# The mixed MLP stage: the fourth block product two block products later, and the seven seats for raw weights dealt three, two and two

## The chip, the cores and the metric

The kernel runs on one core of a Trainium2 chip. The metric is the device time of one execution in microseconds; of several runs the median is taken. The engines are named by their jobs: TensorE (PE in the profile) multiplies matrices, VectorE (DVE) and ScalarE (ACT) work on elements, GpSimd (POOL) and SyncE (SP) here mostly issue transfers. Each engine takes its instructions in the order of its own queue.

## What is computed

One layer of an encoder trunk on 256 tokens of width 2048, in float32: a mixer (three attention-like branches behind one projection), and then the MLP, which is the part that matters here:

```python
hdn = jnp.square(jax.nn.relu(_rms_norm(x, norm_mlp_pre[l]) @ w_mlp_up[l]))
x = x + _rms_norm(hdn @ w_mlp_down[l], norm_mlp_post[l])
```

`w_mlp_up` is 2048 by 8192 and `w_mlp_down` 8192 by 2048. All weights are read once from memory as a stream of blocks of 128 partitions by 1024 float32 (512 KB).

## The kernel before

**Products in split precision.** TensorE multiplies in a rounded format. So each raw weight block is split in two: ScalarE copies it to a rounded `hi` (line 158 or 1379), and VectorE subtracts `hi` from the raw block to get `lo` (159 or 1380). The other operand is split likewise. A product is then three sets of matmuls: `hi` by `hi`, `hi` by `lo`, `lo` by `hi`.

**Up and down halves of the MLP.** The up half makes "heads" of 128 hidden units each. A head takes two half blocks of weights (function `up`: 16 matmuls each, lines 174 to 182, 2.77 us of TensorE), after which `post` brings it through relu and square. Two heads make a pair `m`. The function `forms` makes, of a finished pair, the seven sums and differences that the down half needs, as tiles `fm` (16 buffers, lines 1439 to 1450). For the last eight heads `split3` makes a plain split instead (1461, 1462).

**Block products.** For most of the hidden units the down half multiplies two by two blocks with seven products instead of eight (function `down`). The unit is a quad: four heads by 1024 output columns, with the weight blocks called 11, 12, 21 and 22. The products are called F1 to F7, six matmuls each (lines 1517 to 1519), and each needs one weight block or a sum of blocks. `prep` gets them in this order:

- F3 loads 22 and 12, splits 22, and adds 12 into 22 (VectorE, line 1476).
- F7 loads 11, splits 22 as it then is, adds 11 into 22 (VectorE) and issues a transfer on GpSimd's queue that adds 11 into 12 (`dma_add`, line 1479).
- F1 splits 11.
- F6 loads 21, splits 22, and issues a GpSimd transfer that adds 21 into 22.
- F2 splits 21, F5 splits 12, and F4 splits 22 with all four in it.

F4 is thus the last reader of 22, and waits for the second GpSimd transfer of its quad. The products of one group of quads add up in PSUM banks `Q` (F3, F7, F1 in the ring of four `gps` banks that the heads use too, the others in the ring `mps`). When the last quad of a group is done, `post` of `down` moves them into the result `y` through tiles `junk` (line 1524). There are eight groups, of three or four quads: 28 quads.

**The order of the work.** The mixed stage weaves the heads of the up half, four half blocks a quad at first and at the end sometimes three or two (the list `share`), between the products. The order within a quad is written out by hand in the loop at the end of `hybrid_block`: a list of items, among them `us[0]` to `us[3]` (half blocks), `last4` (F4 of the quad before) and `"old"` (finished pairs whose forms are handed over to the list of small tasks). The driver `drive` does the `prep` of an item two products ahead of its matmuls, and emits two small tasks behind each half block and none behind a product. TensorE's order is this order; on the other engines and queues the framework orders instructions by when it expects them to be ready.

**Where raw blocks lie.** The raw blocks of `down` have seats. The function `seat` has two buffers for each of three roles: 22, 12 and 11. A seventh seat is half of a spare tile, `spare[1][:, 0]`, called `sp` in the profile. The function `braw` (line 1360 on) picks the seat and issues the load on SP's queue (line 1369). Before the change 22 and 12 have two seats each, and 11 and 21 together take turns on three: two of role 11 and the spare one (the counter `made`). A load waits until the block that had its seat has been read for the last time. The half blocks of the up weights are loaded on the same SP queue, into a ring of three buffers called `raw` (line 145).

Of the kernel before, what the change touches and what calls it, by code (L numbers as in the profile page):

```python
# [10 lines left out]
F32 = mybir.dt.float32  # L11
# [39 lines left out]
def hybrid_block(ctx, tc, xt, x, gains, params, consts, lora, gup, wst, out):  # L51
# [13 lines left out]
    def nm(s):  # L65
        uid[0] += 1
        return f"{s}_{uid[0]}"
# [7 lines left out]
    def pk():  # L75
        return pkpool.tile([128, 512], F32R, tag="pk", name=nm("pk"), bufs=24)
# [1144 lines left out]
    def seat(role, dt):  # L1221
        return p2.tile([128, HALF], dt, tag=f"raw{role}", name=nm(f"raw{role}"), bufs=2)
# [72 lines left out]
    for k2 in range(0, KT, 2):  # L1295
        turned(k2, 1)
        src = [trs[k2 // 2][:, i * T:i * T + T] for i in range(2)]
        us = [pk(), pk()]
# [29 lines left out]
    ahead, spare, made, kinds, units = [AHEAD], [], [0], [0], [0]  # L1328
# [31 lines left out]
    def braw(h0, c0, n):  # L1360

        i, j = int(n[0]) - 1, int(n[1]) - 1
        u = base + 64 * (h0 // 16) + 32 + 8 * (c0 // 512 + j) + h0 % 16 // 2
        if n in ("22", "12"):
            raw = seat(int(n), F32)
        else:
            made[0] += 1
            raw = seat(11, F32) if made[0] % 3 else spare[1][:, 0]
        nc.sync.dma_start(out=raw.rearrange("p (r c) -> p r c", r=2),
                          in_=wst[u:u + 2, :, 512 * i:512 * i + 512].rearrange("r p c -> p r c"))  # L1370
        return raw
# [62 lines left out]
    def forms(m):  # L1434

        def sums():
            h = hid[m]
            s = hid[m, 1] = p2.tile([128, 4, 128], F32, tag="sfm", name=nm("sfm"), bufs=1)
            V.tensor_tensor(s[:, 0:2], h[:, 0:4:2], h[:, 3:4].to_broadcast([128, 2, 128]), ALU.subtract)
            V.tensor_tensor(s[:, 2], h[:, 0], s[:, 1], ALU.add)  # L1440
            V.tensor_tensor(s[:, 3], s[:, 2], h[:, 1], ALU.subtract)
            fmh[m] = fm()
            A.activation(fmh[m][:, 0:3], h[:, 0:3], AF.Copy)
            A.activation(fmh[m][:, 3:7], s, AF.Copy)

        def low():
            h, s, hi = hid.pop(m), hid.pop((m, 1)), fmh[m]
            lo = fml[m] = fm()
            V.tensor_tensor(lo[:, 0:3], h[:, 0:3], hi[:, 0:3].bitcast(F32), ALU.subtract)
            V.tensor_tensor(lo[:, 3:7], s, hi[:, 3:7].bitcast(F32), ALU.subtract)  # L1450

        return [(("fm", m), sums), (("fm", m), low)]

    def split3(m):

        def half(i):
            h = hid[m]
            t = fm().rearrange("p a b -> p (a b)")[:, 0:512]
            src = h[:, 0:4:3] if i == 0 else h[:, 1:3]
            hi = t[:, 0:T].rearrange("p (s t) -> p s t", s=2)  # L1460
            A.activation(hi, src, AF.Copy)
            V.tensor_tensor(t[:, T:].rearrange("p (s t) -> p s t", s=2), src, hi.bitcast(F32), ALU.subtract)
            hp[2 * m + i] = t

        return [(("fm", m), lambda i=i: half(i)) for i in range(2)]

    def down(b, sb):
# [13 lines left out]
        def prep(f, d):  # L1481

            h0 = FIRST[b] + 4 * d
            if f == 3:
                R[d, "22"], R[d, "12"] = braw(h0, c0, "22"), braw(h0, c0, "12")
                r = parts(R[d, "22"])
                add(R[d, "22"], R[d, "12"])
            elif f == 7:
                R[d, "11"] = braw(h0, c0, "11")
                r = parts(R[d, "22"])  # L1490
                add(R[d, "22"], R[d, "11"])
                dma_add(R[d, "12"], R[d, "11"])
            elif f == 1:
                r = parts(R[d, "11"])
            elif f == 6:
                R[d, "21"] = braw(h0, c0, "21")
                r = parts(R[d, "22"])
                dma_add(R[d, "22"], R[d, "21"])
            elif f == 2:
                r = parts(R[d, "21"])  # L1500
            elif f == 5:
                r = parts(R[d, "12"])
            else:
                r = parts(R[d, "22"])
            return r
# [56 lines left out]
    def later(new):  # L1562
        return (None, lambda _: urgent.append(lambda: tasks.extend(new)), 0)
# [20 lines left out]
    old = []  # L1584
    last4 = None
# [5 lines left out]
    for b in range(4):  # L1591
        for sb in range(2):
            for d, F in enumerate(down(b, sb)):
                us = [halves.pop(0) for _ in range(share.pop(0))]
                new = [j // 2 for i, (u, j) in enumerate(us) if j % 2 and (u, j) == halves_of[j]]
                us = [u for u, j in us] + [None] * 4
                last = b == 3 and sb == 1 and d == SIZES[3] // 4 - 1
                for it in (F[3], us[0], last4, "old", F[7], F[1], us[1], F[6], F[2], us[2], F[5], us[3]):
                    if it == "old":
                        keep = []  # L1600
                        for m in old:
                            if m in left:
                                work.append(later(split3(m) if m >= LAST else forms(m)))
                            else:
                                keep.append(m)
                        old[:] = keep
                    elif it:
                        work.append(it[:2] + (1,) if last and it[2] == 0 else it)
                old.extend(new)
                last4 = F[4]  # L1610
                if sb:
                    for m in (2 * d, 2 * d + 1):
                        left[FIRST[b] // 2 + m + 8] = 0
# [195 lines left out]
```

## Time and profile before

| | |
|---|---|
| median of 3 runs | 1491.31 us (1491.28 to 1491.65) |
| the profiled execution | 1493.0 us, of which the span from first to last instruction is 1491.2 us |
| mean granted TensorE clock | 0.998 |
| memory read, written | 282.65 MB, 4.19 MB |
| loads of raw blocks on SP's queue | 497 of 512 KB, 4.4 us from issue to landing (median) |
| adding transfers on GpSimd's queue | 38 and 18 of 512 KB, 7.4 and 7.6 us |

How to read the lines that follow. A row of a timeline has the start in us, the time in us, the engine, the line of the kernel, the operation, what it writes and reads, and in brackets how long the engine stood idle before it and who ended that. A row of the waits has who waited for whom, the total in us, how often, and the longest. A row of the chain of waits has the start, the time and what it was. A row of a table by stretches has, for a stretch from A to B us, the busy time of each engine with its number of instructions, then the granted clock, the share of the DMA engines and GB/s. Ends of matmuls are modelled and overlap, so gaps on TensorE are measured from start to start.

### The profile page before, as it was taken

The numbers are of one execution on the slowest core, as the hardware profiler recorded it, in microseconds if no ns is written. First come the engines' busy times: TensorE is split into PE (matmuls) and PEld (weight loads), VectorE is DVE, ScalarE is ACT, GpSimd is POOL, SyncE is SP. The second block draws the span as 40 slices with busy tenths as digits, with TensorE's granted clock in tenths as the row PEclk, the third lists the DMA queues.
The fourth block names the chain that finished last, engine by engine and source line by source line (L and its number), as shares of the span: only waits on it lengthen the run. The fifth ranks groups of instructions, "written<-read, shape, count | busy, mean of one in ns | idle before, by whom it ended". The sixth has DMA issues, their size and how long they took to land.

```text
span 1491.2 us, 22865 instructions
## 1 busy us (share of the span) xinstructions
PE 1477.0 (99%) x8427; PEld 1247.7 (84%) x8427; DVE 1214.7 (81%) x1688; ACT 933.1 (63%) x1394; POOL 90.0 (6%) x160
## 2 busy tenths in 40 slices
PE   9999999999999999999999999999999999999997
PEld 8888888888778888788888888888888888888885
DVE  7676778999778898567647788989899989999996
ACT  7465666654576554474445777777767767767663
POOL 0011000100001100000000000000000000100000
PEclk9999999999999999999999999999999999999999
DMA  7545454545445545445756768888888987889974
GB/s 286 186 163 184 160 179 169 182 162 197 174 148 167 183 167 203 144 161 185 269 196 224 257 215 244 242 268 235 267 258 248 271 255 221 258 259 270 272 242 151
DMA packets 107759, 317.70 MB, mean 213 GB/s; under 512 B 10752, under 2 KB 14976, under 8 KB 107392
## 3 DMA queue, kind: packets, MB, share of 16 engines
q1 hardware_dynamic: 94688, 284.39, 55.0%
q0 software_dynamic: 8064, 29.36, 10.4%
q10 hardware_dynamic: 4896, 2.49, 0.6%
q8 instruction: 66, 1.08, 0.3%
q14 instruction: 45, 0.37, 0.1%
HBM read 282.65 MB, written 4.19 MB: 192 GB/s over the span
## 4 chain that ended last, share of the span: by engine, by line
PE 76%; issue 20%; DVE 2%; DMA 1%; ACT 0%; POOL 0%; POOLq 0%; DVEq 0%; SPq 0%; ACTq 0%
PE gps L220 28%; PE gps L174 16%; PE gps L178 9%; PE gps L204 7%; PE mps L1517 1%; PE mps L1518 1%; PE mps L1519 1%; PE gps L182 1%; PE gps L1517 1%; PE gps L1519 1%; PE gps L1518 1%; PE gps L340 1%; DMA raw<-raw 1%; DMA raw<-in_wst_dram 1%; DVE wlo L159 1%
## 5 line engine op out<-in xcount | busy, mean ns | idle before, releaser
L159 DVE TENSOR_TENSOR wlo<-raw,whi 128x1024 fp32r<-128x1024 f32 x501 | 608.1, 1222 | 157.2 <-ACT whi L158 141.5
L158 ACT ACTIVATE whi<-raw 128x1024 fp32r<-128x1024 f32 x501 | 527.7, 1057 | 258.8 <-DMA raw<-in_wst_dram 89.6
L174 PE MATMUL gps<-pk,whi 128*128 128x512 f32 x1321 | 332.6, 391 | 0.7 <-DVE junk L1524 0.7
L220 PE MATMUL gps<-whi,pk 128*128 128x512 f32 x1136 | 286.4, 392 | 0.0
L174 PEld LDWEIGHTS gps<-pk,whi 128*128 128x128 f32 x1321 | 244.5, 188 | 48.9 <-ACT pk L1418 1.0
L220 PEld LDWEIGHTS gps<-whi,pk 128*128 128x128 f32 x1136 | 211.3, 188 | 44.2 <-issue 0.4
L178 PEld LDWEIGHTS gps<-pk,wlo 128*128 128x128 f32 x1408 | 192.0, 190 | 13.7
L178 PE MATMUL gps<-pk,wlo 128*128 128x256 f32 x1408 | 196.9, 282 | 0.0
L220 PE MATMUL gps<-wlo,pk 128*128 128x512 f32 x568 | 155.2, 392 | 0.0
L220 PEld LDWEIGHTS gps<-wlo,pk 128*128 128x128 f32 x568 | 105.7, 188 | 22.0
L1380 DVE TENSOR_TENSOR sp<-raw,sp 128x1024 fp32r<-128x1024 f32 x71 | 86.7, 1221 | 5.6 <-ACT sp L1379 5.4
L1379 ACT ACTIVATE sp<-raw 128x1024 fp32r<-128x1024 f32 x71 | 74.9, 1055 | 16.4 <-PE mps L1519 4.3
L1408 ACT ACTIVATE sp<-gps 128x512 f32<-128x512 f32 x52 | 31.1, 598 | 83.0 <-PE gps L182 83.0
L204 PE MATMUL gps<-whi,pk 128*128 128x512 f32 x256 | 68.9, 390 | 0.0
L1517 PE MATMUL mps<-whi,fm 128*128 128x512 f32 x168 | 66.1, 394 | 0.0
L1518 PE MATMUL mps<-whi,fm 128*128 128x512 f32 x168 | 65.8, 392 | 0.0
L1519 PE MATMUL mps<-wlo,fm 128*128 128x512 f32 x168 | 65.5, 390 | 0.0
L1479 POOL DMA_DIRECT2D raw<-raw x38 | 33.2, 874 | 410.1 <-DVE raw L1476 131.5
L1476 DVE TENSOR_TENSOR raw<-raw,raw 128x1024 f32<-128x1024 f32 x47 | 57.3, 1220 | 0.4
L204 PEld LDWEIGHTS gps<-whi,pk 128*128 128x128 f32 x256 | 47.8, 188 | 9.9
L1517 PE MATMUL gps<-whi,fm 128*128 128x512 f32 x126 | 49.2, 391 | 0.0
L1519 PE MATMUL gps<-wlo,fm 128*128 128x512 f32 x126 | 49.1, 390 | 0.0
(398 smaller groups left out, 1983.3 us busy)
## 6 DMA issues: line engine op xcount, KB each, us to landing
raw<-in_wst_dram SPq DMA_DIRECT2D x497, 512.0 KB, 4.4
raw<-raw POOLq DMA_DIRECT2D x38, 512.0 KB, 7.4
sp<-in_wst_dram SPq DMA_DIRECT2D x18, 512.0 KB, 4.7
raw<-sp POOLq DMA_DIRECT2D x18, 512.0 KB, 7.6
x<-in_x_dram SPq DMA_DIRECT2D x8, 256.0 KB, 6.2
xs<-x SPq DMA_DIRECT2D x2, 1024.0 KB, 7.2
x<-xs SPq DMA_DIRECT2D x4, 512.0 KB, 6.1
out_dram<-x SPq DMA_DIRECT2D x7, 256.0 KB, 2.7
```

The lines of the kernel that those rows point to most:

```text
L158: A.activation(hi, raw, AF.Copy)
L159: V.tensor_tensor(lo, raw, hi.bitcast(F32), ALU.subtract)
L174: PE.matmul(ps, hi[:, i * 128:i * 128 + 128], pks[i], start=first and i == 0, stop=False)
L178: PE.matmul(ps[:, 0:T], lo[:, i * 128:i * 128 + 128], pks[i][:, 0:T], start=False, stop=False)
L204: PE.matmul(ps[tt], pks[k][:, c:c + 128], w[:, (k - k0) * 512:(k - k0) * 512 + 512], start=k == 0 and part == 0 and w is hl[0], stop=w is ...
L220: PE.matmul(ps[tt], pks[k][:, c:c + 128], w[:, (k - k0) * 512:(k - k0) * 512 + 512], start=k == 0 and part == 0 and w is hl[0], stop=False)
L1379: A.activation(hi, raw, AF.Copy)
L1380: V.tensor_tensor(lo, raw, hi.bitcast(F32), ALU.subtract)
L1476: V.tensor_tensor(x, x, z, ALU.add)
L1517: PE.matmul(Q[f], p, w, start=d == 0 and i == 0, stop=False)
L1518: PE.matmul(Q[f], pl, w, start=False, stop=False)
L1519: PE.matmul(Q[f], p, wl, start=False, stop=d == nd - 1 and i == 1)
```

## The change

The change has two parts. In the hand-written order, F4 of the quad before (`last4`) moves from behind the first half block to behind F7 and F1, just ahead of the second half block; `"old"` keeps its place in the list and so now stands directly behind the first half block. And in `braw` the counter now counts loads of 22: every third 22 goes to the spare seat, so 22 takes turns on three seats; 12 keeps its two; 11 and 21 share the two seats of role 11.

```diff
@@ -1361,11 +1361,11 @@
 
         i, j = int(n[0]) - 1, int(n[1]) - 1
         u = base + 64 * (h0 // 16) + 32 + 8 * (c0 // 512 + j) + h0 % 16 // 2
-        if n in ("22", "12"):
-            raw = seat(int(n), F32)
+        made[0] += n == "22"
+        if n == "22" and made[0] % 3 == 0:
+            raw = spare[1][:, 0]
         else:
-            made[0] += 1
-            raw = seat(11, F32) if made[0] % 3 else spare[1][:, 0]
+            raw = seat({"22": 22, "12": 12}.get(n, 11), F32)
         nc.sync.dma_start(out=raw.rearrange("p (r c) -> p r c", r=2),
@@ -1595,7 +1595,7 @@
                 last = b == 3 and sb == 1 and d == SIZES[3] // 4 - 1
-                for it in (F[3], us[0], last4, "old", F[7], F[1], us[1], F[6], F[2], us[2], F[5], us[3]):
+                for it in (F[3], us[0], "old", F[7], F[1], last4, us[1], F[6], F[2], us[2], F[5], us[3]):
                     if it == "old":
```

## The prediction

> **What bounds the kernel now.** I read the page first, then a table by stretches of the mixed stage (it runs from 879.4 to 1435 us), then who made TensorE wait inside it.
>
> ```profile
> span 1491.2 us, 22865 instructions
> ...
> PE 1477.0 (99%) x8427; PEld 1247.7 (84%) x8427; DVE 1214.7 (81%) x1688; ACT 933.1 (63%) x1394; POOL 90.0 (6%) x160
> ```
>
> ```profile
> core 0: us, PE busy (x) PEld busy (x) DVE busy (x) ACT busy (x) POOL busy (x), PEclk, DMA share, GB/s
> 879.40:1389.00 509.60, 509.60 (x2603) 435.90 (x2602) 473.43 (x552) 363.01 (x484) 43.43 (x50) 1.00 0.85 251
> 1389.00:1391.00 2.00, 1.35 (x7) 0.83 (x5) 2.00 (x3) 2.00 (x4) 0.00 (x0) 1.00 0.99 365
> 1391.00:1435.00 44.00, 44.00 (x225) 37.59 (x224) 40.44 (x46) 29.29 (x41) 4.35 (x5) 1.00 0.88 253
> ```
>
> ```profile
> PE gps L174 <- DVE junk L1524: 0.7, 1, 0.7
> ```
>
> TensorE is busy for the whole of 509.60 us and the whole of 44.00 us, at full clock, and loses time in one place of 2 us between them. The third fence is everything that its list of waits holds for this stage: one wait. VectorE is the next engine, 473.43 of 509.60 us (93%); ScalarE is at 71%. Since ends of matmuls are modelled, I measure the one hole by starts:
>
> ```profile
> 1385.55 0.40 PE L1517 MATMUL mps<-whi,fm 128*128 128x512 f32 x1
> ...
> 1388.74 0.39 PE L1519 MATMUL gps<-wlo,fm 128*128 128x512 f32 x1
> ...
> 1389.19 0.39 PE L1518 MATMUL gps<-whi,fm 128*128 128x512 f32 x1
> 1389.42 0.39 PE L1519 MATMUL gps<-wlo,fm 128*128 128x512 f32 x1
> 1390.46 1.86 PE L174 MATMUL gps<-pk,whi 128*128 128x512 f32 x7 [0.65 <-DVE junk L1524]
> ```
>
> Neighbouring 512-wide matmuls start 0.23 apart (1389.19, 1389.42); the last row starts 1.04 after its forerunner, so the hole is 1.04 - 0.23 = 0.81 us. That is all that this change can win in the stage it touches, 0.05% of the run. Anything under 0.2% (3 us) can't be told from no change by a measurement of this kernel.
>
> **Where the 0.81 us come from.** The chain of waits across the hole:
>
> ```profile
> 1372.07 9.76 DMA raw<-raw
> ...
> 1381.92 1.07 ACT whi L158
> ...
> 1383.01 0.04 DVE wlo L159
> ...
> 1388.50 1.22 DVE wlo L159
> 1389.72 0.61 DVE junk L1524
> ```
>
> ```profile
> 1381.92 1.06 ACT L158 ACTIVATE whi<-raw 128x1024 fp32r<-128x1024 f32 x1 [2.36 <-DMA raw<-raw]
> 1382.88 1.05 ACT L1379 ACTIVATE sp<-raw 128x1024 fp32r<-128x1024 f32 x1
> 1383.83 1.04 ACT L158 ACTIVATE whi<-sp 128x1024 fp32r<-128x1024 f32 x1
> ...
> 1388.94 1.05 ACT L1379 ACTIVATE sp<-raw 128x1024 fp32r<-128x1024 f32 x1
> ```
>
> ```profile
> 1383.01 1.22 DVE L159 TENSOR_TENSOR wlo<-raw,whi 128x1024 fp32r<-128x1024 f32 x1 [0.86 <-ACT whi L158]
> ...
> 1385.89 1.22 DVE L1476 TENSOR_TENSOR raw<-raw,sp 128x1024 f32<-128x1024 f32 x1
> 1387.03 1.22 DVE L159 TENSOR_TENSOR wlo<-sp,whi 128x1024 fp32r<-128x1024 f32 x1
> ...
> 1389.63 0.68 DVE L1524 TENSOR_TENSOR junk<-junk,gps 128x512 f32<-128x512 f32 x1
> ...
> 1391.36 1.22 DVE L1380 TENSOR_TENSOR sp<-raw,sp 128x1024 fp32r<-128x1024 f32 x1
> ```
>
> The GpSimd-issued transfer that adds block 21 into block 22 was issued at 1372.07 and landed at 1381.83. The split of that 22 for the fourth product is the ScalarE row at 1381.92: ScalarE had stood idle 2.36 us for it. Behind it on ScalarE's queue stood the splits of the next quad's seventh (1382.88) and first (1383.83) products, which need nothing of that transfer. VectorE lost 0.86 us in turn, and its accumulation that frees a PSUM bank (1389.63, ending 1390.31) came too late for the half block at 1390.46. How near the edge VectorE was is also seen in the first product: its low part was ready at 1387.03 + 1.22 = 1388.25 and TensorE read it at 1388.74, 0.5 us later.
>
> **Part one: the fourth product two products later.** It issues no DMA and no add: six matmuls, one split on ScalarE (1.06) and one on VectorE (1.22). All stay; they are moved behind the seventh and first products' splits and the add of 11 into 22, past no instruction of SP or GpSimd. From 1385.55 six matmuls of about 0.23 are one product, 1.36 us; two of them move the fourth to 1388.27, 2.72 us later, and its split may wait until 1381.92 + 2.72 = 1384.64 with the same lead as now. The landing at 1381.83 is then 2.8 us ahead instead of 0.09 behind. The splits of the seventh and first products take up ScalarE's idle 2.36 us, and VectorE's 0.86 us of waiting goes. The bank-freeing accumulation ends 0.86 earlier, at 1389.45; from its end (1390.31) to the start of the matmuls (1390.46) it took 0.15, so TensorE could go on at 1389.60, and without a hole it would want to at 1389.42 + 0.23 = 1389.65. That just closes the hole. Bounds: -0.81 us, and 0 if VectorE finds other work ahead of that accumulation; I take -0.7.
>
> What is late next: the first product's split is now due 1.36 us nearer to the half block before it. From that half block to the end of the first product's split VectorE has three operations of 1.22 (split, the add at 1385.89, split: 3.66) in two products' 2.72 us, before four (4.88) in three products' 4.08. The lead falls by 0.9 instead of 0.8 there: 0.1 more, against the 0.5 left at the worst place, which itself grows by the 0.86. I put it at nothing; without that lead it would cost 0.1 us in a quad.
>
> The list of finished pairs whose forms are to be made ("old") now stands right after the first half block. Forms are still handed out after the second half block, so nothing is emitted sooner, but they write `fm` tiles that the fourth product reads until 2.72 us later:
>
> ```profile
> ACT fm L1443 <- PE mps L1518: 1.8, 5, 0.4
> ...
> ACT whi L158 <- DMA raw<-raw: 2.4, 1, 2.4
> ```
>
> Five times ScalarE already waits for that read, 0.4 us at most. A gain is excluded: the read only comes later. Bounded by nothing, if splits that are ready go ahead, and by 5 x 2.72 = 13.6 us, if ScalarE stands still and no lead is left. I take nothing: the splits due in the same slot need no `fm` tile and can fill the wait.
>
> **Part two: the places.** Seats for raw blocks stay seven. Block 22 gets three in turn, 12 keeps two, 11 and 21 share two instead of three. A 22 may then be loaded one quad sooner, which moving its last reader by 2.72 us would otherwise have made later. A 21 now takes the seat of the 21 before it, free when the add of that 21 into 22 has landed; before, it took the seat of an 11, free one GpSimd add (half a quad) sooner. Each half quad SP stands at one such landing, before and after:
>
> ```profile
> SPq L1369 <- DMA raw<-raw: 179.9, 35, 8.3
> SPq L1369 <- DMA raw<-sp: 89.3, 17, 8.1
> ```
>
> 52 waits for 28 quads, two per quad less the ends. Behind the waiting load on SP's queue stand the second half's raw loads of the up weights; the change swaps which load waits (21 of the next quad where 11 of the one after stood), not how long. So they cost nothing new. What shrinks is the time from landing to use:
>
> ```profile
> 1361.47 0.38 SPq L1369 DMA_DIRECT2D sp<-in_wst_dram  x1
> ...
> 1381.85 0.89 SPq L1369 DMA_DIRECT2D raw<-in_wst_dram  x2
> ```
>
> ```profile
> DMA to landing us min/median/max: 3.8/6.8/10.8
> ```
>
> (The second fence: these block loads between 1300 and 1436.) At 1381.85 the slot was freed in the quad of the hole. A 21 loaded then lands at 1388.7 with the median time, and ScalarE splits it at 1388.94: 0.3 us in hand, or -0.5 once the hole is gone. At 1361.47 it would land at 1368.3; the fence below has the two splits, of which the second (start 1370.36, one 1.08 after the first) needs it, 2.1 in hand.
>
> ```profile
> 1369.27 2.16 ACT L158 ACTIVATE whi<-raw 128x1024 fp32r<-128x1024 f32 x2 [1.07 <-PE mps L1519]
> ```
>
> Lateness is absorbed by the lead of the split over TensorE, so I put this part at 0, with bounds 0 and the price of the rival below.
>
> The Trainium skill, page "DMA: Bandwidth & Descriptors", section "Anatomy of one DMA — SWDGE (gpsimd) path", gives 2.0 us plus bytes over 436 GB/s for such a transfer; my estimate from it is 3.2 us for these 512 KB. By that the add would have landed at 1375.3, the split would never have waited, and the sum would be 0. The trace disagrees: 9.76 us here.
>
> **Sum.** The profiled execution took 1493.0 us, its span 1491.2 and 1.8 around it; -0.7 makes a span of 1490.5. The runs shown have the median 1491.31 (1491.28 to 1491.65), so the same step gives 1490.6.
>
> **Rivals.** *The hole stays or moves* (1491.3): VectorE at 93% has no reserve, and 0.86 us just closes 0.81; any other order on its queue reopens it. For: the margin of 0.05. Against: 553.6 us of this stage run at the same load without a hole. Chance 0.17.
>
> *Slower, by late 21 blocks.* The place is 21's shared seat, the price is lateness less lead. A load of the longest time, 10.8, would land at 1392.65, 3.7 after the split is due; the low part (VectorE, 1391.36 to 1392.58) is read at 1395.17, 2.6 later, so a hole of about 1.1 us.
>
> ```profile
> 1395.17 0.39 PE L1519 MATMUL mps<-sp,fm 128*128 128x512 f32 x1
> ```
>
> It decides from a load of 1388.94 + 2.6 - 1381.85 = 9.7 us on. So tight are only the quads behind a short one (fewer than four half blocks): the schedule has seven short ones, 7 x 1.1 = 7.7 us, 1490.6 + 7.7 = 1498.3. For: DMA is at 0.85 to 0.99 here. Against: the median of 6.8. Chance 0.07, of which 0.05 beyond 3 us.
>
> *ScalarE waits for `fm` tiles.* Five places, each 0.4 + 2.72 us of waiting less the lead of 2.6 measured above: 5 x 0.5 = 2.5 us, 1493.1. Chance 0.08, of which 0.01 beyond 3 us.
>
> *TensorE has more to give* than its hole: were it bound by how early its operands come, the 73.7 us by which weight loads fall short of 509.60 would be open, and time could fall by more than 3 us, to 1488 or less. Against: starts stand 0.23 apart wherever the leads are short or long. Chance 0.02. The Trainium skill, page "Perfetto Trace Analysis", section "Identifying the Most-Contended Engine", would judge headroom by just that weight-load share, 86% here, and not by matmul busy time; the spacing of starts speaks against it.
>
> **How the numbers follow.** The forecast has 0.66. The range goes from 1490.2 (the whole 0.81, and the spread of the runs) to 1492.8 (hole unclosed, and most of the `fm` waits). Faster than 0.2%: 0.02. Slower: 0.05 + 0.01 = 0.06. The rest, 0.92, lies within.
>
> **What would show it.** Right: the wait of a half block for the accumulation in "junk" is gone; so is ScalarE's wait of 2.4 for the add's landing; loads of 22 are issued a quad sooner; SP's waits for GpSimd landings stay near 270 us in total. Wrong: TensorE waiting in product rows (L1517 to L1519) of the second product behind a split that waited for a load, or ScalarE's waits in L1443 of 2 to 3 us with TensorE waiting after them.

## The result and the profile after

The changed kernel takes 1500.71 us in the median of six runs (1499.82 to 1508.07); the kernel before, run beside it, 1491.66 us (1491.28 to 1492.36). The ratio is 1.0066, 95% interval 1.0056 to 1.0076: some 9 us slower. The profiled execution took 1500.67 us.

The page of the changed kernel, the head and the row of the engines:

```profile
span 1498.9 us, 22869 instructions
...
PE 1479.0 (99%) x8427; PEld 1247.6 (83%) x8427; DVE 1215.3 (81%) x1688; ACT 931.7 (62%) x1394; POOL 90.0 (6%) x160
```

The number of matmuls is that of before and the busy times nearly so; 7.7 us of span have come in as waiting. The table by stretches says where (the first stretch has the same bounds as before):

```profile
879.40:1389.00 509.60, 502.32 (x2560) 427.91 (x2559) 465.35 (x544) 354.93 (x476) 42.59 (x49) 1.00 0.84 248
...
1399.00:1443.00 44.00, 44.00 (x225) 37.60 (x224) 40.50 (x46) 30.07 (x42) 4.35 (x5) 1.00 0.91 258
```

TensorE, busy for all of the first stretch before, now lacks 7.28 us there. The list of TensorE's waits for the stage has again a single row, but another one:

```profile
PE gps L174 <- ACT sp L1408: 7.3, 5, 2.5
```

Five times the first matmul of `us[0]`, the first half block of a quad (u0 from here on), waits for line 1408, ScalarE's copy that brings a finished head out of its PSUM bank; u0 opens a new head and needs that bank. From start to start the five holes are 0.68, 2.66, 1.66, 1.79 and 1.30 us, 8.1 together; less the old hole of 0.81, which is gone, that is 7.3 of the 7.7 us.

ScalarE's list of waits shows what stands behind the copy. First three rows of before, then four of after, for the same stretch of 870 to 1450 us:

```profile
ACT whi L158 <- DMA raw<-in_wst_dram: 8.0, 5, 2.8
...
ACT whi L158 <- DMA raw<-raw: 2.4, 1, 2.4
...
ACT whi L158 <- DVE raw L1476: 1.1, 3, 0.5
```

```profile
ACT whi L158 <- DMA raw<-in_wst_dram: 19.5, 10, 3.3
ACT whi L158 <- DVE raw L1476: 18.5, 9, 3.0
...
ACT sp L1379 <- DMA raw<-in_wst_dram: 8.4, 4, 3.2
...
ACT whi L158 <- DVE sp L1476: 7.3, 3, 3.7
```

The wait for GpSimd's adding transfer (2.4) is gone, as foretold. In its place ScalarE waits longer for loads, and, new, for VectorE's line 1476: the add of 12 into 22, which F7's split needs.

**The largest hole, followed back.** ScalarE, VectorE and TensorE of the changed kernel there:

```profile
1022.39 1.06 ACT L158 ACTIVATE whi<-raw 128x1024 fp32r<-128x1024 f32 x1 [3.12 <-DMA raw<-in_wst_dram]
1023.36 0.62 ACT L1444 ACTIVATE fm<-sfm 128x512 fp32r<-128x512 f32 x1
1025.94 1.06 ACT L158 ACTIVATE whi<-raw 128x1024 fp32r<-128x1024 f32 x1 [1.96 <-DVE raw L1476]
1026.90 0.58 ACT L1408 ACTIVATE sp<-gps 128x512 f32<-128x512 f32 x1
```

```profile
1023.49 1.23 DVE L159 TENSOR_TENSOR wlo<-raw,whi 128x1024 fp32r<-128x1024 f32 x1 [2.46 <-ACT whi L158]
1024.63 1.22 DVE L1476 TENSOR_TENSOR raw<-raw,raw 128x1024 f32<-128x1024 f32 x1
```

```profile
1027.54 0.73 PE L174 MATMUL gps<-pk,whi 128*128 128x512 f32 x2 [2.50 <-ACT sp L1408]
```

Read it as one chain. u0's load is late; ScalarE splits u0 (1022.39); VectorE makes its low part (1023.49) and only then the add (1024.63), which stands behind it; ScalarE's next split is F7's (1025.94), which needs the add; behind it stands the copy (1026.90 to 1027.48); then TensorE can begin u0 (1027.54). From the start of u0's split to the end of the copy pass 5.09 us. The same place in the kernel before, in its quad with the latest u0, ScalarE and VectorE:

```profile
979.05 1.06 ACT L158 ACTIVATE whi<-raw 128x1024 fp32r<-128x1024 f32 x1 [2.45 <-DMA raw<-in_wst_dram]
980.02 1.04 ACT L1379 ACTIVATE sp<-raw 128x1024 fp32r<-128x1024 f32 x1
981.69 0.60 ACT L1408 ACTIVATE sp<-gps 128x512 f32<-128x512 f32 x1 [0.63 <-PE gps L182]
982.60 1.06 ACT L158 ACTIVATE whi<-raw 128x1024 fp32r<-128x1024 f32 x1 [0.31 <-DVE raw L1476]
```

```profile
980.14 1.23 DVE L159 TENSOR_TENSOR wlo<-raw,whi 128x1024 fp32r<-128x1024 f32 x1 [2.28 <-ACT whi L158]
981.29 1.22 DVE L1476 TENSOR_TENSOR raw<-raw,raw 128x1024 f32<-128x1024 f32 x1
```

u0's load was late there too, and the add stood behind it too. But between u0's split and the copy stood F4's split (980.02), which needs nothing of u0; the copy came behind that, and waited for TensorE itself (0.63). F7's split with its wait for the add came after the copy. F4 was the cover, and the change took it away.

**Two numbers per quad.** The quads below are named by about the time when TensorE was due to start u0. Call *lead* the time from the start of u0's split to the moment when TensorE is due to start u0 (the start of F3's first matmul + 1.36 us), and *need* the time from that split to the end of the copy where nothing else holds the copy. The hole should be need - lead + 0.06 (0.06 from the copy's end to the matmul):

| quad with a hole, after | lead | 5.09 - lead + 0.06 | hole |
|---|---|---|---|
| at 982 | 4.45 | 0.70 | 0.68 |
| at 1025 | 2.46 | 2.69 | 2.66 |
| at 1110 | 3.47 | 1.68 | 1.66 |
| at 1133 | 3.32 | 1.83 | 1.79 |
| at 1155 | 3.82 | 1.33 | 1.30 |

Not every late u0 has such a hole. Four quads whose u0 starts at 1069.06, 1219.06, 1239.76 and 1373.46 have leads of 4.50, 3.59, 4.09 and 3.98 and no hole. In them VectorE does the add ahead of u0's low part, so F7's split follows u0's at once, and the copy waits for TensorE alone. ScalarE and VectorE in the one with the shortest lead:

```profile
1215.45 1.06 ACT L1379 ACTIVATE sp<-raw 128x1024 fp32r<-128x1024 f32 x1 [3.19 <-DMA raw<-in_wst_dram]
1216.42 1.04 ACT L158 ACTIVATE whi<-raw 128x1024 fp32r<-128x1024 f32 x1
1217.88 0.60 ACT L1408 ACTIVATE sp<-gps 128x512 f32<-128x512 f32 x1 [0.42 <-PE gps L182]
```

```profile
1213.56 1.23 DVE L1476 TENSOR_TENSOR raw<-raw,raw 128x1024 f32<-128x1024 f32 x1
1216.55 1.22 DVE L1380 TENSOR_TENSOR sp<-raw,sp 128x1024 fp32r<-128x1024 f32 x1 [1.76 <-ACT sp L1379]
```

So 5.09 is the need where the add stands behind u0's low part. And in a quad that is the first of its group u0 did not wait for this copy: at 1004 the lead is 3.92, the copy ends at 1005.18, and u0 has begun at 1004.02 without a hole.

Before, the shortest leads were 3.80, 4.31 and 4.51, the second of them in the first quad of a group. With the need of 5.09 the other two would have cost at most 1.35 + 0.64 = 2.0 us. So there are two losses: the need has grown, and the leads have shrunk. For the second, SP's queue and its waits around the hole at 1025:

```profile
1002.31 1.14 SPq L145 DMA_DIRECT2D raw<-in_wst_dram  x2
1014.02 0.38 SPq L1369 DMA_DIRECT2D raw<-in_wst_dram  x1
1014.49 1.20 SPq L1369 DMA_DIRECT2D sp<-in_wst_dram  x1
1015.79 0.61 SPq L145 DMA_DIRECT2D raw<-in_wst_dram  x1
```

```profile
SPq L1369 <- DMA raw<-raw: 10.5, 1, 10.5
```

SP stands 10.5 us at an 11 (1014.02) that waits for a GpSimd add to land; behind it come a 22 (1014.49) and then u0 (1015.79), whose load takes until 1022.31. The order in which the kernels issue the loads of a full quad, read from their instruction lists (u0 to u3 are the half blocks, ' the next quad, * a load that waits for a GpSimd landing):

```
before       22   21*  u0  u1   11'* 12'  u2  u3
after        11*  22'  u0  u1   21*  12'  u2  u3
order only   21*  22   u0  u1   11'* 12'  u2  u3
seats only   22'  11*  u0  u1   21*  12'  u2  u3
```

Nobody wrote this order: the framework makes it from when it expects things to be ready. Before, 22 was issued ahead of the load that waits; now it comes behind it, and takes its share of the transfers in just the time in which u0 is fetched.

### The profile page after: what moved, and what is told of

Read it like the earlier page. It is cut to its first block, busy times and chain, and to the rows that moved or that the text cites. A ratio compares the mean times of both kernels' runs of the same rounds, so it can differ in the third digit from the quotient of the medians.

```text
span 1498.9 us, 22869 instructions
## 1 busy us (share of the span) xinstructions
PE 1479.0 (99%) x8427; PEld 1247.6 (83%) x8427; DVE 1215.3 (81%) x1688; ACT 931.7 (62%) x1394; POOL 90.0 (6%) x160
## 3 DMA queue, kind: packets, MB, share of 16 engines
q10 hardware_dynamic: 4896, 2.49, 0.6%
## 4 chain that ended last, share of the span: by engine, by line
PE 93%; DMA 3%; DVE 2%; issue 1%; ACT 1%; SPq 0%; POOLq 0%; POOL 0%; DVEq 0%; ACTq 0%
PE gps L220 28%; PE gps L174 22%; PE gps L178 12%; PE gps L204 7%; PE mps L1517 3%; PE mps L1518 3%; PE mps L1519 3%; PE gps L1517 2%; PE gps L1518 2%; PE gps L1519 2%; DMA raw<-in_wst_dram 2%; PE gps L182 1%; PE mps L828 1%; PE gps L340 1%; DVE wlo L159 0%
## 5 line engine op out<-in xcount | busy, mean ns | idle before, releaser
L159 DVE TENSOR_TENSOR wlo<-raw,whi 128x1024 fp32r<-128x1024 f32 x488 | 592.1, 1221 | 161.5 <-ACT whi L158 145.7
L158 ACT ACTIVATE whi<-raw 128x1024 fp32r<-128x1024 f32 x488 | 513.7, 1056 | 266.9 <-DMA raw<-in_wst_dram 93.3
L174 PE MATMUL gps<-pk,whi 128*128 128x512 f32 x1321 | 333.0, 392 | 5.6 <-ACT sp L1408 5.6
L174 PEld LDWEIGHTS gps<-pk,whi 128*128 128x128 f32 x1321 | 244.3, 188 | 55.0 <-ACT sp L1408 7.3
L1380 DVE TENSOR_TENSOR sp<-raw,sp 128x1024 fp32r<-128x1024 f32 x66 | 80.4, 1219 | 10.3 <-ACT sp L1379 10.2
L1379 ACT ACTIVATE sp<-raw 128x1024 fp32r<-128x1024 f32 x66 | 69.6, 1055 | 20.3 <-DMA raw<-in_wst_dram 8.4
L1479 POOL DMA_DIRECT2D raw<-raw x47 | 41.0, 873 | 499.0 <-DVE raw L1476 143.2
L1517 PE MATMUL mps<-whi,fm 128*128 128x512 f32 x168 | 65.9, 392 | 0.0
L174 PE MATMUL gps<-pk,sp 128*128 128x512 f32 x194 | 48.3, 390 | 1.6 <-ACT sp L1408 1.6
L1517 PE MATMUL gps<-whi,fm 128*128 128x512 f32 x126 | 49.5, 393 | 0.0
L1518 PE MATMUL gps<-whi,fm 128*128 128x512 f32 x126 | 49.2, 391 | 0.0
```

Source lines behind the costliest of these rows:

```text
L158: A.activation(hi, raw, AF.Copy)
L159: V.tensor_tensor(lo, raw, hi.bitcast(F32), ALU.subtract)
L174: PE.matmul(ps, hi[:, i * 128:i * 128 + 128], pks[i], start=first and i == 0, stop=False)
L1379: A.activation(hi, raw, AF.Copy)
L1380: V.tensor_tensor(lo, raw, hi.bitcast(F32), ALU.subtract)
L1479: G.dma_start(out=x, in_=z, accum_op=ALU.add)
```

## The experiments

Theory A: the loss needs both, a chain behind u0 without cover and a u0 that is late. The rivals stand with each run. Each was timed beside the kernel before; ratios are to that, with the 95% interval.

**1. The order alone.** The new place of `last4`, the old seats.

```diff
-for it in (F[3], us[0], last4, "old", F[7], F[1], us[1], F[6], F[2], us[2], F[5], us[3]):
+for it in (F[3], us[0], "old", F[7], F[1], last4, us[1], F[6], F[2], us[2], F[5], us[3]):
```

> The new order (F4 two products later) with the old seats. Theory A (order): F7's split stands directly behind u0's on ScalarE, waits for the add behind u0's low part, and holds the copy that frees the PSUM bank of the next head; it costs whenever u0's load is late, and SP's order here (a 21 that waits for a landing, then 22, then u0) leaves u0 as late as in the changed kernel: 1496 to 1502 us, TensorE's wait in L174 for ScalarE's L1408 there, 3 to 8 times. Theory B (seats): the seats alone make the loss, the order is free as predicted: 1490.5 to 1491.7 us and no such wait.

1514.35 us against 1492.25, ratio 1.0148 (1.0123 to 1.0173): slower than either theory said. Its waits of TensorE and of ScalarE for loads:

```profile
PE gps L174 <- ACT sp L1408: 8.9, 7, 2.2
PE gps L1517 <- ACT whi L158: 3.7, 2, 2.0
```

```profile
ACT whi L158 <- DMA raw<-in_wst_dram: 43.8, 19, 7.0
```

Theory B falls: the order alone costs 22 us. The holes in L174 are there, seven of them, 10.0 us from start to start in the profiled execution (1519.51 us), and in four of them the need is 5.09 or 5.10 again (the one at 982 has a lead of 3.34, so 1.81 against 1.78 measured). What A had not seen is a second loss of about the same size, in rows of products: in the list above this kernel issues 22 behind the load that waits, and F3 of the same quad needs it at once. TensorE waits in F3's first row (L1517) for a split that waited up to 7 us for a load.

**2. The seats alone.** The other line of the change, with the old order.

> The new seats (three, two, two) with the old order. Theory A (order): F4's split stands between u0's and F7's, and the copy L1408 behind F4's; a late u0 costs nothing: 1490.5 to 1492.5 us, no wait of TensorE in L174 for L1408. Theory B (seats): the loss of the changed kernel stays, 1498 to 1501 us, with late u0 or late 21 blocks.

1492.36 us against 1492.25, ratio 1.0000 (0.9991 to 1.0010). TensorE's list of waits for the stage is empty. B falls here as well: the seats alone cost nothing.

**3. The copy first.** In the changed kernel the tasks of a finished head are emitted ahead of the next splits, and F7's split is tied behind the copy on ScalarE.

```diff
+            now, urgent[:] = urgent[:], []
+            for f in now:
+                f()
             for w in [(prep, run, n)] + [w for w in work if w[0]][:ahead[0]]:
...
-            now, urgent[:] = urgent[:], []
             run(hl.pop((prep, run, n)))
-            for f in now:
-                f()
...
-                r = parts(R[d, "22"])
+                with tc.issue_after(freed[0].ins):
+                    r = parts(R[d, "22"])
```

> The changed kernel, but the finished head's PSUM copy (L1408) is put ahead of F7's split on ScalarE; loads, seats and TensorE's order stay. Theory A (order): TensorE's waits in L174 for L1408 are gone though u0's loads are as late as before: 1490.5 to 1492.5 us. Theory C (lateness itself): u0's late load holds TensorE by its own split, whatever stands behind it: 1496 to 1501 us, with the waits named L158 or L159 in place of L1408.

1504.96 us against 1492.25, ratio 1.0083 (1.0068 to 1.0098). TensorE's waits (its lines are further down: 1524 here is 1519, 1409 is 1408):

```profile
PE gps L1524 <- DVE wlo L159: 4.1, 4, 1.9
PE mps L1524 <- DVE wlo L159: 2.3, 4, 1.0
...
PE gps L174 <- ACT sp L1409: 0.3, 1, 0.3
```

A's first half holds: the wait for the copy falls from 7.3 to 0.3 us. Its forecast of the time fails: the waits are now mostly for low parts of the products, nine holes of 8.3 us together out of 10.6 us. Moving the copy does not shorten the chain from u0 through the add to F7; it moves what the end of the chain reaches. C named L159, but for u0's own low part; these are rows of products.

**4. F1 before F7.** In the changed kernel F1 and F7 exchange places, and F1 loads 11.

```diff
-for it in (F[3], us[0], "old", F[7], F[1], last4, us[1], F[6], F[2], us[2], F[5], us[3]):
+for it in (F[3], us[0], "old", F[1], F[7], last4, us[1], F[6], F[2], us[2], F[5], us[3]):
...
             elif f == 7:
-                R[d, "11"] = braw(h0, c0, "11")
...
             elif f == 1:
+                R[d, "11"] = braw(h0, c0, "11")
```

> The changed kernel with F1 and F7 exchanged (F1 loads and splits 11, F7 follows it, F4 still two products later than in the kernel before): an independent split stands between u0's and F7's again. Theory A (order): the copy L1408 comes behind F1's split and no longer behind the add; no such hole: 1490.5 to 1492.5 us. Theory C (lateness itself): 1496 to 1501 us. Against both: block 11 is now wanted one product sooner, and if its load is late there, 1493 to 1496 us with ScalarE waiting for it.

1493.67 us against 1492.25, ratio 1.0006 (0.9997 to 1.0016). u0 is no earlier (shortest lead 2.01), and ScalarE waits for loads longer than in the changed kernel, but TensorE loses 0.8 us in all:

```profile
ACT whi L158 <- DMA raw<-in_wst_dram: 28.6, 15, 3.5
```

```profile
PE gps L174 <- ACT sp L1408: 0.3, 1, 0.3
```

C falls: with a split behind u0 that depends on nothing of u0 the need is 2.49 (the larger hole has a lead of 2.01: 2.49 - 2.01 + 0.06 = 0.54 against 0.51), and the same lateness is nearly free. The time lies 1.2 us above A's range and in that of the third forecast; but ScalarE's longest waits for loads, the four over 2.5 us in the stage, are for u0 and not for block 11.

**5. The same with the old seats.**

> F4 two products later, F1 before F7, old seats: what the fourth experiment had, without the change of seats. Theory A (order): the holes behind u0 (in the kernel with the order alone some 11 us of TensorE, in L174) go, the late loads of 22 stay (some 10 us, TensorE waiting in F3's rows for a split that waited for a load): 1498 to 1504 us. Theory D (the exchange heals all): 1491 to 1493 us, as with the new seats.

1500.5 us against 1492.03, ratio 1.0056 (1.0041 to 1.0071). D falls, A is right on the time and half right on the rest: waits in L174 remain (2.8 us in 4), beside those for late 22 blocks. The third seat for 22 is worth some 7 us with this order, where it was worth nothing with the old one.

**6. u0 early.** The changed kernel, whose loads alone are tied otherwise: the next quad's 22 is loaded in F7's `prep`, and 11 behind it. SP then issues 22', u0, 11*, u1.

```diff
             elif f == 7:
-                R[d, "11"] = braw(h0, c0, "11")
+                pre[quads[k]] = braw(*quads[k], "22")
+                with tc.issue_after(issued[0].ins):
+                    R[d, "11"] = braw(h0, c0, "11")
```

> The changed kernel, but on SP's queue the next quad's 22 is put ahead of the 11 that waits for a landing, which also lets u0's load go ahead of that wait; the orders on TensorE and ScalarE stay. Theory A (late u0 and what stands behind it): no hole in L174 any more, ScalarE's waits for half blocks' loads fall from 19.5 us to under 6: 1490.5 to 1493 us. Theory E (the order is too tight by itself, lateness or not): 1496 to 1501 us, L174 waiting for L1408 as before.

1491.70 us against 1492.03, ratio 0.9998 (0.9988 to 1.0007). The table by stretches and ScalarE in the quad of the largest hole:

```profile
879.40:1389.00 509.60, 509.60 (x2603) 435.86 (x2602) 475.66 (x553) 362.38 (x484) 43.43 (x50) 1.00 0.87 252
```

```profile
1017.23 1.06 ACT L158 ACTIVATE whi<-raw 128x1024 fp32r<-128x1024 f32 x1 [0.50 <-PE gps L174]
...
1020.77 1.06 ACT L158 ACTIVATE whi<-raw 128x1024 fp32r<-128x1024 f32 x1 [1.97 <-DVE raw L1476]
1022.34 0.60 ACT L1408 ACTIVATE sp<-gps 128x512 f32<-128x512 f32 x1 [0.50 <-PE gps L182]
```

The chain is as it was, 1.97 us of waiting for the add included; it only starts with a lead of 6.27 us, and the copy waits for TensorE and not TensorE for the copy. E falls. TensorE's order is that of the changed kernel, the new place of `"old"` included, and the edit touches only the loads on SP's queue; the whole loss is gone.

**7 and 8. The add first.** In the changed kernel VectorE's add of 12 into 22 is put ahead of u0's low part (7); and the copy ahead of F7's split besides (8).

```diff
-                add(R[d, "22"], R[d, "12"])
+                added12[:] = [add(R[d, "22"], R[d, "12"])]
...
+        with tc.issue_after(added12.pop().ins):
+            return split(raw)
```

> The changed kernel, but VectorE adds 12 into 22 ahead of u0's low part, so that F7's split no longer depends on u0's load; the order on ScalarE and on SP stays. Theory A (chain behind a late u0): F7's split follows u0's without a wait, the copy L1408 comes up to 2 us earlier, and of the holes (0.7, 2.7, 1.7, 1.8, 1.3) only some 0.7 us of the second stays: 1491.5 to 1493.5 us. Theory F (the two splits ahead of the copy are enough): holes as before, 1498 to 1501 us.

> The changed kernel with both: the add ahead of u0's low part, and the copy L1408 ahead of F7's split. Theory A: F7's low part, which was late where the copy alone was put ahead, no longer waits for u0: 1491 to 1493 us, no waits of TensorE in F7's rows. Theory F: as with the copy alone, 1503 to 1506 us.

1494.83 and 1494.56 us against 1492.03, ratios 1.0016 (1.0006 to 1.0026) both. TensorE's waits in 7:

```profile
PE gps L174 <- ACT whi L158: 0.9, 1, 0.9
PE gps L174 <- ACT sp L1408: 0.5, 1, 0.5
```

F falls for both: two thirds of the loss go by cutting the chain at the add, with SP's order untouched. In 7 u0 is as late as in the changed kernel (four quads with leads of 2.82 to 3.49 have no hole), and the hole at 1025 is 0.65 us, as forecast (need 3.94, lead 3.32). Both end above the range that A gave; in 7 there is also a hole of 1.06 us at a half block whose own split is late. The runs of 8 go from 1491.28 to 1497.52, and its profiled one (1492.86) has a single hole of 0.56 us, so what the slower of them lose the profile doesn't show.

**9. The old order with a late u0.** The kernel of experiment 2, whose loads are tied in the sequence of the changed kernel (11*, 22', u0): F3's `prep` also loads 11 and, tied behind it, the next quad's 22, and u0's load is tied behind that (`upraw`).

```diff
-                R[d, "22"], R[d, "12"] = braw(h0, c0, "22"), braw(h0, c0, "12")
+                R[d, "22"], R[d, "12"], R[d, "11"] = early(h0, c0)
...
+        r = [pre.pop(q) if q in pre else braw(*q, "22"), braw(*q, "12"), braw(*q, "11")]
+            with tc.issue_after(load[0].ins):
+                pre[quads[k]] = braw(*quads[k], "22")
...
+        with tc.issue_after(load.pop().ins):
+            return wraw(n)
```

> The old order with the new seats, and on SP's queue the order of the changed kernel (11 that waits for a landing, then the next quad's 22, then u0), so that u0's load is as late as there. Theory A (a late u0 costs only if nothing stands between it and F7): 1491 to 1494 us, ScalarE's waits for half blocks' loads near the 19.5 us of the changed kernel, at most one small hole in L174. Theory G (SP's order makes the loss whatever the order of the products): 1497 to 1501 us.

1505.65 us against 1492.26, ratio 1.0091 (1.0076 to 1.0106): outside both, and against A as it was put. ScalarE at its first large hole:

```profile
1024.41 1.06 ACT L158 ACTIVATE whi<-raw 128x1024 fp32r<-128x1024 f32 x1 [4.00 <-DMA raw<-in_wst_dram]
1025.38 0.61 ACT L1444 ACTIVATE fm<-sfm 128x512 fp32r<-128x512 f32 x1
1025.90 1.04 ACT L158 ACTIVATE whi<-raw 128x1024 fp32r<-128x1024 f32 x1
1026.84 0.57 ACT L1408 ACTIVATE sp<-gps 128x512 f32<-128x512 f32 x1
```

F4's split (1025.90) follows without a wait and the copy behind it; with the 0.61 us of line 1444 between, the need is 3.00 here, and 2.49 where nothing is between. But the lead was only 0.39. The next large hole has 0.30, and 2.49 - 0.30 + 0.06 = 2.25 against 2.22 measured. So the rule of need and lead holds for these holes, with a need of 2.49; they are 5.9 us of some 11.5, and the others stand at half blocks and products whose own operands or banks are late. The run did not have the lateness that I meant to give it but a greater one (ScalarE waits 44.4 us for loads into `whi`), why is not settled. So it does not decide between A and G. It shows that the sequence of loads alone can cost 13 us, and that F4 is a cover of 2.6 us (5.09 - 2.49) and no more.

**10. The new order, 22 ahead of the wait.** The changed kernel with the loads tied as 22', 11*, u0.

> The new order with the new seats, and on SP's queue the order of the kernel before in so far as u0 follows a 22 and then the load that waits (here 22, 11 that waits, u0): u0 still stands behind the wait, but no 22 is moved between the landing and u0's load. Theory A, if the 22 ahead of u0 makes most of its lateness: ScalarE's waits for loads 5 to 10 us, holes in L174 1 to 3 us together: 1492 to 1495 us. If the wait for the landing makes it: as the changed kernel, 1498 to 1501 us.

1494.63 us against 1492.26, ratio 1.0018 (1.0008 to 1.0027), 2.4 us.

```profile
PE gps L174 <- ACT sp L1408: 1.4, 2, 0.8
```

The two holes in L174 have leads of 4.39 and 4.12: 5.09 - 4.39 + 0.06 = 0.76 against 0.73, and 1.03 against 1.00. So the greater need alone, with leads near the shortest of before, costs about the 2.0 us worked out above; the other 6 to 7 us of the loss go when 22 is loaded ahead of the wait. That is the first branch of the expectation for the time, but not for ScalarE's waits, which were 25.7 us and not 5 to 10. u0 is late nearly as often: counted over all splits, u0's wait 12 times for their loads, 22.0 us, against 11 times and 24.4 us in the changed kernel and 3 times and 6.5 us before. What differs is the lead in the quads with four half blocks, at least 3.87 here against 2.46. How much of u0's lateness the 22 makes and how much the wait for the landing is therefore not settled.

## Why the prediction was wrong

The forecast was 1490.6 us, and the range to 1492.8. By its own steps:

- **The bound** (TensorE, one hole of 0.81 us to be won). Right. Experiments 2 and 6 have no hole left in the stage and take the time of before within 0.1%. The 3 us under which I said nothing can be told from no change were too many: experiments 7, 8 and 10 tell 2.4 to 2.8 us from nothing.
- **The old hole closes** (-0.7). It is gone, as forecast: no wait for `junk`, no wait of ScalarE for the landing, in the profile after. That the move closed it is not shown, for experiment 2, with the old order, has no hole there either.
- **Part one, "I put it at nothing; without that lead it would cost 0.1 us in a quad".** This step failed. I asked whose lead the move shortens and found F1's split; I did not ask what F4's own split had been standing in front of. It stood between u0's split, which often waits for a load, and F7's, which waits for an add behind u0's low part; and the copy that frees u0's bank stood behind the first of the two. Without it the need rises from 2.49 us (experiment 9) to 5.09, where VectorE's add stands behind u0's low part; the five holes of 8.1 us come from there. I had quoted that ScalarE's splits were held up by one late transfer, and took the splits behind it as work free to fill the gap; one of them was tied to a late load itself. And I worked from the one quad with a hole, the first of a group, where u0 waits for `junk` and not for the copy.
- **"Past no instruction of SP or GpSimd".** Failed too. The product issues no DMA, but the seat that it frees is waited for by a load of 22, and the framework moved that load behind the one that waits for a landing. Alone (experiment 1) this makes 22 late for F3; with the third seat it makes u0 late. The loss needs both failures: of the 9 us, 2.8 are left where only the chain is cut (7), 2.4 where only 22 is loaded ahead of the wait (10), and none where u0 is loaded ahead of it as well (6).
- **Part two at 0.** Right alone (experiment 2). With part one it is not 0: it takes back 1514 to 1501, because 22 is then loaded a quad ahead. "Not how long" holds for the seats alone (53 waits of SP for landings, 272.4 us, in experiment 2) and not for the whole change: 52 waits of 269.2 us became 53 of 321.5:

```profile
SPq L1369 <- DMA raw<-raw: 263.5, 44, 10.5
...
SPq L1369 <- DMA sp<-raw: 58.0, 9, 9.2
```

- **The rivals.** The late 21 blocks (1498.3) come near the time by chance: TensorE waits nowhere in rows of products. ScalarE's waits for `fm` tiles (L1443) did not grow; they are gone. Neither sign that I had named as proof against me appeared; the one that did, SP's waits well over 270 us, I had listed as a sign of right or wrong but given no price.

## What to carry to other kernels

Before an item is moved in an ordered queue, write down what stands in front of it and behind it there, and what each of the two waits for: an item that depends on nothing late is cover for all that stands behind it, whatever it is worth itself. A buffer that becomes free later moves the load that waits for it, and every load behind that one; where a framework sets the order of the queue, look at that order before pricing the change at nothing. And put a lead and a need beside each other for the operand that is latest already: here their difference gave the holes behind u0 within 0.05 us in the changed kernel and in experiments 4, 7, 9 and 10 (in experiment 1 two of seven were smaller than it by 0.2 and 0.9 us).

## What was not expected of the hardware

The same adding transfer of 512 KB landed after very different times: from 4.8 to 11.4 us in the stage before (median 7.5), from 4.7 to 11.1 after (8.0). A load of 512 KB issued on SP's queue took 4.1 to 10.9 us between 1000 and 1020 us of the profile after, within one quad. Against leads of 2.5 to 6 us such a spread can decide from quad to quad whether there is a hole. That it makes the runs of kernels with short leads scatter is not shown: those of experiment 1 go from 1509.86 to 1519.51 and of 8 from 1491.28 to 1497.52, those of experiment 6 only from 1491.28 to 1492.36, but five of the six of the changed kernel lie within 1.0 us, the sixth at 1508.07.
